# Scores by exchanged parts of q instead of k: buffers, 128-row loads, mix by quarters and an early copy of x in a hybrid attention layer

## The chip, the cores and the metric

The kernel runs on one core of a Trainium2 chip. The metric is the device time of one execution in microseconds. TensorE is called PE (its weight loads PEld), VectorE DVE, ScalarE ACT, GpSimd POOL; SP (SyncE) issues most of the transfers, POOL some of them.

## The reference

One layer: a norm, one wide projection, eight heads of differential attention and four heads of gated linear attention side by side, a gate and a norm on each, the output projection, a norm, and the residual. All arrays are float32, 1024 positions of 1024 columns.

```python
h = rms_norm(x, pre_g)
z = jnp.einsum('bsd,de->bse', h, w_in)
qa, ka, va, ga, qb, kb, vb, gb, gk_low = split_columns(z)
...
# diff_attention: q, k hold two maps of 64 columns per head
s = jnp.einsum('bqhmd,bkhmd->bhmqk', qb, k).astype(jnp.float32)   # q scaled by 64 ** -0.5
p = jax.nn.softmax(jnp.where(mask, s, -jnp.inf), axis=-1)         # causal
w = p[:, :, 0] - lam * p[:, :, 1]
out = jnp.einsum('bhqk,bkhv->bqhv', w.astype(v.dtype), v)
...
oa = rms_norm(oa, subln_g) * (1.0 - lam_init)
oa = oa.reshape(B, S, DA_WIDTH) * jax.nn.silu(ga)
ob = gla_chunked(qb, kb, vb, log_a)        # gated linear attention
ob = rms_norm(ob, gla_g) * jax.nn.silu(gb)
y = jnp.einsum('bse,ed->bsd', jnp.concatenate([oa, ob], axis=-1), w_out)
return x + rms_norm(y, post_g)
```

## The kernel before

**Two parts of every number.** A float32 value enters PE as two parts, `hi` (rounded) and `lo` (the rest); a product takes hi*hi + lo*hi + hi*lo. For the scores the two parts lie beside each other along the contracted side: a q or k of 64 columns becomes 128 rows, its hi in rows 0 to 63 and its lo in rows 64 to 127. `k` has the order hi, lo; `ks` is the same k with the order lo, hi. A score tile is `q` times `k` (hi*hi + lo*lo) plus `q` times `ks` (hi*lo + lo*hi); `q` is the stationary operand in both (`scores`, L1128).

**Stages.** First x is loaded, normed and transposed, and projected by a scheme of seven products on 2x2 blocks (`order`, `go`, `step`): the values of the linear attention (VB), those of the attention (VA), and then q, k and gates in pairs of heads. `take` (L366) splits finished q and k into parts and stores them in DRAM, in `qk_d`, laid out [part, map, 64, position]: one store for each part, 128 rows (both maps) of 512 positions, or one store for both parts in the last steps. The linear attention (`gla`) is mingled with the last projections. From about 617 us on come the heads of the attention: three streams are merged in a written order (`merge`): the scores (`all_scores`), the values (`all_values`), and the output projection of what is finished (`out_early`), which keeps PE busy between them. At the end, the partial results are summed, normed and added to x.

**Loads of a head.** `load_qk` (L979) loads one half (512 positions) of `q`, `k` or `ks` into a tile of 128 rows: two transfers of 64 rows each, one for each part, of 256 KB. A head works down from its last block of 128 queries (`qb` 7) to its first; half 1 of q serves blocks 7 to 4, half 0 blocks 3 to 0, and every block needs k from position 0 on. Even heads use the tags of the pool `kp`; odd heads have their own tiles (`smps`) for k0, k1, ks0 and q1. The tags ks1 and q0 have one buffer for all heads: ks1 is loaded once the head before has done block 4, q0 once it has done block 0.

**Output projection.** `load_mix` (L1335) loads finished attention outputs from `mixd`, four rows of tiles by 512 positions, into `m_raw`, one buffer; `mix_part` splits them. The order of output blocks is `ENDS` = 4, 5, 6, 7, 0, 1, 2, 3. `weights` (L1008) loads the output weights (`wo_hi`, `wo_lo`). The residual gets to the output by a copy of x to `out` from DRAM to DRAM, for six blocks; at the end their results are added to it by accumulating transfers. The copies are written in `out_early`, on SP (L1393).

**Order.** All matmuls, and what goes through `keep_in_program_order`, keep the order of the code; among these on SP are the last stores of q and k, the first two loads of `mix`, the last `wo` loads, and v of head 0. All else is ordered by the framework's scheduler, which follows its own model of time. Each queue then works in its fixed order.

Of the kernel before, what the change touches and what calls it, by code (L numbers as in the profile page):

```python
# [14 lines left out]
P = 128  # L15
# [16 lines left out]
def hymba_kernel(  # L32
# [181 lines left out]
    def load_early(p):  # L214

        c0 = pairs[p][2]
        r = kp.tile([P, 2, HB, P], F32, tag=f"ks{p % 2}", name="w_early")
        early[p] = [r[:, 0], r[:, 1]]
        for kh in range(2):
            rows = slice(kh * 512, kh * 512 + 512)  # L220
            sp.dma_start(r[:, kh], w_in[0, rows, c0 : c0 + P].rearrange("(k p) c -> p k c", p=P))
# [44 lines left out]
    def block_weights(i):  # L266

        kind, n, kk = order[i]
        b11, b12, b21, b22, t = (
            blocks_w.get((kind, name, kk)) for name in ("11", "12", "21", "22", "t")  # L270
        )
        w = [ap.tile([P, 2, 512], F32R, tag="ring", name="w", bufs=NRING) for _ in range(2)]
        with in_turn():
            if n == 6:
                t = kp.tile([P, 2, 512], F32, tag=f"ks{kk}", name="w_t")
# [9 lines left out]
            act.copy(w[0], src)  # L285
            split_last[:] = [dve.tensor_tensor(w[1], src, fp(w[0]), ALU.subtract)]
        ws[i] = w
        if (kind, n, kk) == ("VB", 7, 1):
            make_blocks("VA", "11", ("k0", "k1"))
            load_blocks("VA", "11")  # L290
        elif (kind, n, kk) == ("VB", 4, 1):
            make_blocks("VA", "12", None)
            make_blocks("VA", "21", None)
            make_blocks("VA", "22", ("q0", "q1"))
            load_blocks("VA", "21", "12", "22")
        elif (kind, n, kk) == ("VA", 7, 1):
            load_raw(0)
        elif (kind, n, kk) == ("VA", 4, 1):
            load_raw(1)
# [66 lines left out]
    def take(kind, n, half, unit, c):  # L366

        cs = cols(half)
        if kind in ("QA", "KA"):
            h = n + unit  # L370

            ending = made[0] > len(order) - LEAD
            both = None
            if ending and order[made[0] - 1][1] == 7:
                both = ap.tile([P, 2, 512], F32R, tag="raw", name="qk_st", bufs=4)
                hi, lo = both[:, 0], both[:, 1]
            else:
                hi, lo = t_st("qk_st", F32R), t_st("qk_st", F32R)
            scale = -0.125 if kind == "QA" else 1.0
            act.activation(hi, c, AF.Copy, scale=scale)  # L380
            dve.scalar_tensor_tensor(lo, c, scale, fp(hi), ALU.mult, ALU.subtract)
            d = qk_d["q" if kind == "QA" else "k"][h]
            if both is not None:
                tc.keep_in_program_order(
                    sp.dma_start(d[:, :, :, cs].rearrange("t m p s -> (m p) t s"), fp(both))
                )
            else:
                for t, src in enumerate((hi, lo)):
                    ins = sp.dma_start(d[t, :, :, cs].rearrange("m p s -> (m p) s"), fp(src))
                    if ending:  # L390
                        tc.keep_in_program_order(ins)
        elif kind in ("GA", "GB"):
            g = t_st("g_st")
            act.activation(g, c, AF.Exp, scale=-1.0)
            act.activation(g, g, AF.Ln, bias=1.0)
            act.activation(g, g, AF.Exp, scale=-1.0)
            dve.tensor_tensor(g, c, g, ALU.mult)
            d = g_d[n + unit] if kind == "GA" else gg_d[n][unit]
            sp.dma_start(d[:, cs], g)
        elif kind == "QB":  # L400
            g = n + unit
            e_q, _ = decs[g]
            q, qd = t_st("gq_st"), t_st("gq_st")
            dve.scalar_tensor_tensor(q, c, QSCALE, e_q[:, cs], ALU.mult, ALU.mult)
            dve.tensor_tensor(
                qd.rearrange("p (n i) -> p n i", i=P),
                q.rearrange("p (n i) -> p n i", i=P),
                dsteps[g][:, half * 4 : half * 4 + 4].unsqueeze(2).to_broadcast([P, 4, P]),
                ALU.mult,
            )  # L410
            for t, src in enumerate((q, qd)):
                sp.dma_start(gq_d[g][t, :, cs], src)
        else:
# [324 lines left out]
    gkl = kp.tile([P, S], F32R, tag="ks0", name="gkl")  # L738
    ku = kp.tile([P, 2, 512], F32R, tag="ks1", name="ku")
    up, keep = ku[:, 0], fp(ku)[:, 1]  # L740

    def low_rank():
# [94 lines left out]
    def gla_keys(n):  # L837

        g, half = n // 2, n % 2
        if g < GLA_HEADS and n not in keys:  # L840
            kq = keys[n] = kp.tile([P, 2, 512], F32, tag="ks0", name="kq")
            for i, t in enumerate((2, 0)):
                sp.dma_start(kq[:, i], gq_d[g][t, :, cols(half)])

# [36 lines left out]
    def gla():  # L881
# [6 lines left out]
        for g, half in [(g, half) for g in range(GLA_HEADS) for half in range(2)]:  # L888
# [46 lines left out]
                free.append(ib)  # L935
                yield
            yield
            gates = kp.tile([P, 2, 512], F32, tag="ks1", name="gg")
# [39 lines left out]

    def load_qk(h, n, half):  # L979

        if h % 2 and (n == "k" or (n, half) in (("ks", 0), ("q", 1))):
            t = smps[0].tile([P, 2, 512], F32R, tag=f"{n}{half}", name=f"{n}{half}")
        else:
            t = kp.tile([P, 2, 512], F32R, tag=f"{n}{half}", name=f"{n}{half}")
        for i in range(2):
            d = qk_d["q" if n == "q" else "k"][h][1 - i if n == "ks" else i, :, :, cols(half)]
            sp.dma_start(fp(t[64 * i : 64 * i + 64]), d.rearrange("m p s -> p m s"))
        qk[h, n, half] = t

    qk, smps = {}, []  # L990
# [5 lines left out]
    for _ in fill[0] if fill else ():  # L996
        pass
    fill.clear()
    for n in ("q", "k", "ks"):
        load_qk(0, n, 1)  # L1000
        if n != "q":
            load_qk(0, n, 0)
    load_qk(0, "q", 0)

    E, wo = D // P, {}
    md = mixd.rearrange("(e p) s -> p e s", p=P)
# [121 lines left out]
    def scores(h, qb):  # L1128
# [4 lines left out]
        p0 = pp.tile([P, n], F32, tag=f"p0_{qb}", name="p0", bufs=1)  # L1133
        p1 = smp.tile([P, S], F32, tag="p1", name="p1", bufs=2)
        for m, p in enumerate((p0, p1)):
            q = qk[h, "q", qb // 4][:, m, qc]
            parts = parts_of(n)
            if h == DA_HEADS - 1 and (qb, m) in ((1, 1), (0, 0), (0, 1)):

                parts = [(0, 512)]  # L1140
            for i, (a, b) in enumerate(parts):
                sc = sc_bank("sc", [P, 512])
                for j, name in enumerate(("k", "ks")):
                    for half in range(2):
                        lo, hi = max(a, half * 512), min(b, half * 512 + 512)
                        if lo < hi:
                            mm(
                                sc[:, lo - a : hi - a], q,
                                qk[h, name, half][:, m, lo - half * 512 : hi - half * 512],
                                start=(j == 0), stop=(j == 1),  # L1150
                            )
                e = min(b, n)
# [49 lines left out]
    def all_scores():  # L1202
        for h in range(DA_HEADS):
            for qb in range(NT - 1, -1, -1):
# [1 line left out]
                    yield lambda h=h, qb=qb: (h - 1, qb // 2) in used  # L1206
                yield from scores(h, qb)
                if qb == NT - 1 and h + 1 < DA_HEADS:
                    for n, half in (("q", 1), ("k", 0), ("k", 1), ("ks", 0)):
                        load_qk(h + 1, n, half)  # L1210
                if qb == 4 and h + 1 < DA_HEADS:
                    load_qk(h + 1, "ks", 1)
            if h + 1 < DA_HEADS:
                load_qk(h + 1, "q", 0)
        for _ in range(3):
            scale_scores(None)
        scored.append(True)
# [112 lines left out]

    wop = ctx.enter_context(tc.tile_pool(name="wop", bufs=1, side="right", reuse_waits="tile"))

    halves = {}

    def load_mix(st, e, n):  # L1335
        half = st // 4
        if (half, e) not in halves:
            raw = halves[half, e] = wop.tile([P, 4, 512], F32, tag="m_raw", name="m_raw", bufs=1)
            sp.dma_start(raw[:, :n, :], md[:, e : e + n, cols(half)])
        return halves[half, e][:, :, st % 4 * P : st % 4 * P + P]  # L1340

    def mix_part(st, e, n, raw=None, pool_d=None):

# [34 lines left out]
    def out_early():  # L1378
# [10 lines left out]
            pool.dma_start(yd[0][dh], y_tile(ps[dh]))  # L1389
        for st in range(1, NT - 1):  # L1390
            part, nxt = nxt, mix(st + 1)
            rows = slice(ENDS[st - 1] * P, ENDS[st - 1] * P + P)
            sp.dma_start(out[0, rows, :], x[0, rows, :])  # L1393
            for dh in range(2):
                ps = y_bank(st, dh, "ypart")
                for e in range(E, E + 8):
# [5 lines left out]
        part = nxt  # L1402
        ps = [y_bank(NT - 1, dh, "ypart") for dh in range(2)]
        load_mix(ENDS[0], 0, 4)
        for e in range(E, E + 8):
            for dh in range(2):
                times(ps[dh], part, E, dh, e, E + 7)
# [7 lines left out]
        for n, st in enumerate(ENDS):  # L1415
# [5 lines left out]
                weights(3 + n, kept)  # L1421
            if n + 1 < NT:
                nxt = mix_part(ENDS[n + 1], 0, 4)
            if n == 2:
                load_mix(ENDS[4], 0, 4)
            for dh in range(2):
                ps = y_bank(st, dh, "ypart")
                for e in range(4):
# [209 lines left out]
```

## Time and profile before

| | |
|---|---|
| Time, median of 3 runs | 1001.48 us (999.04 to 1001.82) |
| Profiled execution | 1000.23 us, span 998.5 us |
| PE busy | 963.4 us, 96% of the span |
| DVE, ACT, POOL busy | 739.4, 590.2, 207.2 us |
| Granted PE clock, mean | 0.988 |
| DMA traffic over the span | 220.37 MB, mean 221 GB/s |

The profile is of one execution. "Waited for" tells what released an engine after an idle time. In the tables by stretch, each engine has its busy time in that stretch and, in brackets, how many instructions; PEclk is the granted share of PE's full clock; the DMA share is the mean busy share of the sixteen DMA engines (a little over 1.00 is full), and GB/s what they moved. A timeline row is: start, length, engine, line, operation, tile written<-tiles read, how many. A row of the chain is: start, length, what.

### The profile page before, as it was taken

The page shows a single profiled execution, that of the slowest core. Times are in us where ns is not written, and L with a number is a line of the kernel's source. Part 1 is how long each engine was busy: PE and PEld are TensorE (multiplying, and loading weights), DVE is VectorE, ACT ScalarE, POOL GpSimd, SP SyncE. Part 2 cuts the span into 40 slices and gives each one's busy share as a digit, 9 for nine tenths or more (in the row PEclk, how much of TensorE's full clock was granted, in tenths as well). Part 3 has the DMA queues.
Part 4 walks back from the last instruction along what each step waited for, and adds up shares of the span by engine and source line. Part 5 has one row for each costly group of instructions (what it writes and reads, how often), then busy time and mean ns, then how long its engine had stood idle before and what let it go on. Part 6 is the DMA issues. An engine that isn't in the chain of part 4 may idle for free.

```text
span 998.5 us, 14800 instructions
## 1 busy us (share of the span) xinstructions
PE 963.4 (96%) x4866; PEld 812.0 (81%) x4866; DVE 739.4 (74%) x1450; ACT 590.2 (59%) x1152; POOL 207.2 (21%) x277
## 2 busy tenths in 40 slices
PE   6999999999999999999999999969999999899997
PEld 4888888778888888888888888758888888788775
DVE  5996476889899767877777784637777777677655
ACT  8641232456476467766677662537667668577664
POOL 5320000012112221211200000213322324343232
PEclk9999999999999999999999999979999999999999
DMA  8644333757857766889975679985596699984657
GB/s 299 228 146 148 127 106 94 229 190 255 299 179 244 270 206 233 273 304 307 299 242 174 189 257 357 316 232 173 161 269 177 166 285 284 296 241 89 178 149 157
DMA packets 142508, 220.37 MB, mean 221 GB/s; under 512 B 14448, under 2 KB 74864, under 8 KB 142336
## 3 DMA queue, kind: packets, MB, share of 16 engines
q1 hardware_dynamic: 128288, 178.53, 57.3%
q0 software_dynamic: 14144, 40.90, 13.8%
q8 instruction: 38, 0.62, 0.3%
q14 instruction: 38, 0.31, 0.1%
HBM read 133.93 MB, written 88.60 MB: 223 GB/s over the span
## 4 chain that ended last, share of the span: by engine, by line
PE 84%; DMA 11%; DVE 3%; ACT 2%; issue 1%; SPq 0%; DVEq 0%; POOL 0%; ACTq 0%
PE x L111 16%; PE v L111 15%; PE y L111 10%; PE z L111 10%; PE ypart L111 9%; PE sc L111 5%; PE po L111 4%; PE yps L111 4%; DMA m_raw<-mixd 3%; PE gpo L111 3%; PE wtr L114 2%; PE kv L111 1%; DMA ks<-k_d 1%; DMA q<-q_d 1%; DMA v<-v_d 1%; DMA k_d<-qk_st 1%
## 5 line engine op out<-in xcount | busy, mean ns | idle before, releaser
L1167 ACT ACTIVATE p<-p,stt 128x896 f32<-128x896 f32 (+7 forms) x128 | 99.2, 776 | 57.2 <-DVE stt L1157 44.2
L330 DVE TENSOR_TENSOR w<-w_raw,w 128x512 fp32r<-128x512 f32 x134 | 92.0, 689 | 36.2 <-ACT w L328 36.0
L328 ACT CAST w<-w_raw 128x512 fp32r<-128x512 f32 x134 | 82.7, 620 | 46.7 <-PE y L111 22.7
L1157 DVE CUSTOM_DVE_ANT_0 p<-sc,maskt 128x512 f32<-128x512 f32 (+3 forms) x128 | 74.5, 586 | 40.0 <-PE sc L111 39.2
L1193 POOL TENSOR_SCALAR p<-p,stt,lam 128x1024 f32<-128x1024 f32 (+3 forms) x64 | 56.0, 876 | 226.9 <-DVE stt L1192 222.0
L111 PE MATMUL ypart<-wo_hi,m_hi 128*128 128x512 f32 x192 | 80.4, 419 | 2.1 <-DMA wo_hi<-wo_d 1.5
L111 PE MATMUL y<-h_hi,w 128*128 128x512 f32 x320 | 80.6, 394 | 0.0
L111 PE MATMUL x<-s_hi,w 128*128 128x512 f32 x320 | 80.5, 394 | 0.0
L111 PE MATMUL z<-s_hi,w 128*128 128x512 f32 x320 | 80.4, 393 | 0.0
L111 PE MATMUL v<-w,s_hi 128*128 128x512 f32 x256 | 79.0, 389 | 0.1
L111 PE MATMUL sc<-k,q 128*128 128x512 f32 (+1 forms) x192 | 72.5, 380 | 6.1 <-DVE stt L1157 6.1
L111 PE MATMUL sc<-ks,q 128*128 128x512 f32 (+1 forms) x192 | 68.0, 356 | 9.4 <-DMA ks<-k_d 9.4
L111 PE MATMUL ypart<-wo_lo,m_hi 128*128 128x512 f32 x192 | 76.6, 399 | 0.5 <-DMA wo_lo<-wo_d 0.5
L111 PE MATMUL ypart<-wo_hi,m_lo 128*128 128x512 f32 x192 | 76.3, 398 | 0.0
L479 ACT COPY s<-x 128x512 f32<-128x512 f32 x60 | 35.1, 584 | 65.3 <-PE x L111 65.1
L111 PEld LDWEIGHTS z<-s_hi,w 128*128 128x128 f32 x320 | 59.1, 188 | 11.7
L111 PEld LDWEIGHTS x<-s_hi,w 128*128 128x128 f32 x320 | 59.1, 188 | 11.7
L111 PEld LDWEIGHTS y<-h_hi,w 128*128 128x128 f32 x320 | 59.0, 188 | 11.7
L285 ACT CAST w<-w_block 128x1024 fp32r<-128x1024 f32 x24 | 25.0, 1051 | 66.3 <-PE v L111 43.2
L257 DVE TENSOR_TENSOR w_raw<-w_raw 128x512 f32<-128x512 f32 x80 | 55.2, 690 | 9.8 <-DMA w_raw<-in_w_in_dram 8.8
L111 PE MATMUL v<-w,h_hi 128*128 128x512 f32 x192 | 60.3, 401 | 0.4 <-ACT h_hi L573 0.4
L1235 ACT CAST wt_hi<-wtr 128x512 fp32r<-128x512 f32 (+1 forms) x80 | 43.1, 538 | 25.6 <-PE wtr L114 24.6
(231 smaller groups left out, 2392.3 us busy)
## 6 DMA issues: line engine op xcount, KB each, us to landing
w_raw<-in_w_in_dram SPq DMA_DIRECT2D x40, 512.0 KB, 5.0
w_block<-in_w_in_dram SPq DMA_DIRECT2D x16, 512.0 KB, 4.2
wo_raw<-in_w_out_dram POOLq DMA_DIRECT2D x32, 256.0 KB, 4.2
wo_d<-wo_hi POOLq DMA_DIRECT2D x32, 256.0 KB, 4.3
wo_d<-wo_raw POOLq DMA_DIRECT2D x32, 256.0 KB, 5.1
ks<-k_d SPq DMA_DIRECT2D x32, 256.0 KB, 8.0
k<-k_d SPq DMA_DIRECT2D x32, 256.0 KB, 8.7
q<-q_d SPq DMA_DIRECT2D x32, 256.0 KB, 8.6
```

The source lines that it names most:

```text
L111: tc.keep_in_program_order(pe.matmul(*a, **k))
L114: tc.keep_in_program_order(pe.transpose(dst, src, ident))
L257: dve.tensor_tensor(dst, a, b, ALU.subtract)
L285: act.copy(w[0], src)
L328: act.copy(w[0], src)
L330: split_last[:] = [dve.tensor_tensor(w[1], src, fp(w[0]), ALU.subtract)]
L479: act.copy(b[k], ps)
L1157: ins = dve.tensor_tensor_reduce(p[:, a:e], sc[:, : e - a], maskt[:, NZ + P - (e - a) :] if last else maskt[:, : e - a], 1.0, 3e38 if i == ...
L1167: act.activation(p[:, :n], p[:, :n], AF.Exp, bias=st[:, m : m + 1], scale=-1.0, accum_out=st[:, 2 + m : 3 + m],)
L1193: pool.tensor_scalar(p1[:, :n], p1[:, :n], st[:, 5:6], lam, ALU.mult, ALU.mult)
L1235: act.copy(hi[:, :n], pt[:, :n])
```

## The change

- Scores: the exchanged operand is now q. `qs` is q with the parts in the order lo, hi; a score tile is `q` times `k` plus `qs` times `k`, with q and qs as stationary operands.
- Buffers: odd heads have their own tiles for k0, k1, q1 and qs1, so that all that a head's blocks 7 to 4 need has two buffers; q0 and qs0 have one, and are loaded once the head before has done block 0. The tags ks0 and ks1, which earlier stages use too, are now called qs0 and qs1.
- Layout: `qk_d` is [map, part, 64, position]. `q` and `k` are loaded by one transfer of 128 rows, `qs` by two of 64. Every store of q or k is split in two, one for each map, of 64 rows.
- `load_mix` loads quarters (256 positions) into two buffers, and asks for some of them earlier.
- The six copies of x to `out` are issued by POOL, and written among the steps of the VA stage.

```diff
@@ load_early (and the same tag in block_weights, gkl, ku, gla_keys, gates)
-        r = kp.tile([P, 2, HB, P], F32, tag=f"ks{p % 2}", name="w_early")
+        r = kp.tile([P, 2, HB, P], F32, tag=f"qs{p % 2}", name="w_early")
@@ block_weights
             load_blocks("VA", "21", "12", "22")
+        elif (kind, n) in (("VA", 1), ("VA", 2), ("VA", 6)):
+            st = {1: 4, 2: 6, 6: 0}[n] + kk
+            pool.dma_start(out[0, st * P : st * P + P, :], x[0, st * P : st * P + P, :])
@@ take
             if both is not None:
-                tc.keep_in_program_order(
-                    sp.dma_start(d[:, :, :, cs].rearrange("t m p s -> (m p) t s"), fp(both))
-                )
+                for m in range(2):
+                    tc.keep_in_program_order(
+                        sp.dma_start(
+                            d[m, :, :, cs].rearrange("t p s -> p t s"), fp(both)[64 * m : 64 * m + 64]
+                        )
+                    )
             else:
                 for t, src in enumerate((hi, lo)):
-                    ins = sp.dma_start(d[t, :, :, cs].rearrange("m p s -> (m p) s"), fp(src))
-                    if ending:
-                        tc.keep_in_program_order(ins)
+                    for m in range(2):
+                        ins = sp.dma_start(d[m, t, :, cs], fp(src)[64 * m : 64 * m + 64])
+                        if ending:
+                            tc.keep_in_program_order(ins)
@@ load_qk
-        if h % 2 and (n == "k" or (n, half) in (("ks", 0), ("q", 1))):
+        if h % 2 and (n == "k" or half):
...
-        for i in range(2):
-            d = qk_d["q" if n == "q" else "k"][h][1 - i if n == "ks" else i, :, :, cols(half)]
-            sp.dma_start(fp(t[64 * i : 64 * i + 64]), d.rearrange("m p s -> p m s"))
+        d = qk_d["k" if n == "k" else "q"][h][:, :, :, cols(half)]
+        if n != "qs":
+            sp.dma_start(fp(t), d.rearrange("m t p s -> (t p) m s"))
+        else:
+            for i in range(2):
+                sp.dma_start(fp(t[64 * i : 64 * i + 64]), d[:, 1 - i].rearrange("m p s -> p m s"))
@@ loads of head 0
-    for n in ("q", "k", "ks"):
-        load_qk(0, n, 1)
-        if n != "q":
-            load_qk(0, n, 0)
-    load_qk(0, "q", 0)
+    for n, half in (("q", 1), ("k", 1), ("k", 0), ("qs", 1), ("q", 0), ("qs", 0)):
+        load_qk(0, n, half)
@@ scores
-                for j, name in enumerate(("k", "ks")):
+                for j, name in enumerate(("q", "qs")):
...
-                                sc[:, lo - a : hi - a], q,
-                                qk[h, name, half][:, m, lo - half * 512 : hi - half * 512],
+                                sc[:, lo - a : hi - a], qk[h, name, qb // 4][:, m, qc],
+                                qk[h, "k", half][:, m, lo - half * 512 : hi - half * 512],
@@ all_scores
-                    for n, half in (("q", 1), ("k", 0), ("k", 1), ("ks", 0)):
+                    for n, half in (("q", 1), ("k", 0), ("k", 1), ("qs", 1)):
                         load_qk(h + 1, n, half)
-                if qb == 4 and h + 1 < DA_HEADS:
-                    load_qk(h + 1, "ks", 1)
             if h + 1 < DA_HEADS:
-                load_qk(h + 1, "q", 0)
+                for n in ("q", "qs"):
+                    load_qk(h + 1, n, 0)
@@ load_mix
-        half = st // 4
-        if (half, e) not in halves:
-            raw = halves[half, e] = wop.tile([P, 4, 512], F32, tag="m_raw", name="m_raw", bufs=1)
-            sp.dma_start(raw[:, :n, :], md[:, e : e + n, cols(half)])
-        return halves[half, e][:, :, st % 4 * P : st % 4 * P + P]
+        part = st // 2
+        if (part, e) not in parts_m:
+            raw = parts_m[part, e] = wop.tile([P, 4, 256], F32, tag="m_raw", name="m_raw", bufs=2)
+            sp.dma_start(raw[:, :n, :], md[:, e : e + n, part * 256 : part * 256 + 256])
+        return parts_m[part, e][:, :, st % 2 * P : st % 2 * P + P]
@@ out_early
-            rows = slice(ENDS[st - 1] * P, ENDS[st - 1] * P + P)
-            sp.dma_start(out[0, rows, :], x[0, rows, :])
...
         load_mix(ENDS[0], 0, 4)
+        load_mix(ENDS[2], 0, 4)
...
-            if n == 2:
-                load_mix(ENDS[4], 0, 4)
+            if n % 2 == 0 and n + 4 < NT:
+                load_mix(ENDS[n + 4], 0, 4)
...
         mix_pair(0)
+        load_mix(ENDS[2], 4, 3)
```

More of the change, by code (lines that the diff above doesn't have):

```diff
@@ L274, in block_weights @@
             if n == 6:
-                t = kp.tile([P, 2, 512], F32, tag=f"ks{kk}", name="w_t")
+                t = kp.tile([P, 2, 512], F32, tag=f"qs{kk}", name="w_t")
                 blocks_w[kind, "t", kk] = t
@@ L737, in hymba_kernel @@
     go(2)
-    gkl = kp.tile([P, S], F32R, tag="ks0", name="gkl")
-    ku = kp.tile([P, 2, 512], F32R, tag="ks1", name="ku")
+    gkl = kp.tile([P, S], F32R, tag="qs0", name="gkl")
+    ku = kp.tile([P, 2, 512], F32R, tag="qs1", name="ku")
     up, keep = ku[:, 0], fp(ku)[:, 1]
@@ L840, in gla_keys @@
         if g < GLA_HEADS and n not in keys:
-            kq = keys[n] = kp.tile([P, 2, 512], F32, tag="ks0", name="kq")
+            kq = keys[n] = kp.tile([P, 2, 512], F32, tag="qs0", name="kq")
             for i, t in enumerate((2, 0)):
@@ L937, in gla @@
             yield
-            gates = kp.tile([P, 2, 512], F32, tag="ks1", name="gg")
+            gates = kp.tile([P, 2, 512], F32, tag="qs1", name="gg")
             for t in range(2):
@@ L1135, in scores @@
         for m, p in enumerate((p0, p1)):
-            q = qk[h, "q", qb // 4][:, m, qc]
             parts = parts_of(n)
@@ L1331, in hymba_kernel @@
     wop = ctx.enter_context(tc.tile_pool(name="wop", bufs=1, side="right", reuse_waits="tile"))
-    halves = {}
+    parts_m = {}
     def load_mix(st, e, n):
-        half = st // 4
-        if (half, e) not in halves:
-            raw = halves[half, e] = wop.tile([P, 4, 512], F32, tag="m_raw", name="m_raw", bufs=1)
-            sp.dma_start(raw[:, :n, :], md[:, e : e + n, cols(half)])
-        return halves[half, e][:, :, st % 4 * P : st % 4 * P + P]
+        part = st // 2
[3 more added lines that the diff above has]
+        return parts_m[part, e][:, :, st % 2 * P : st % 2 * P + P]
     def mix_part(st, e, n, raw=None, pool_d=None):
```

## Prediction

> **What bounds the kernel now.** I read the page's head first, then the waits of PE, then the stretches around each wait, and last the queues.
>
> ```profile
> span 998.5 us, 14800 instructions
> PE 963.4 (96%) x4866; PEld 812.0 (81%) x4866; DVE 739.4 (74%) x1450; ACT 590.2 (59%) x1152; POOL 207.2 (21%) x277
> ...
> PEclk9999999999999999999999999979999999999999
> DMA  8644333757857766889975679985596699984657
> ```
>
> PE is busy 96% of the span, so about 35 us of idle are all that a reordering can win, apart from slices at a lower clock. The waits of PE say where:
>
> ```profile
> PE sc L111 <- DMA ks<-k_d: 9.4, 1, 9.4
> PE xT L114 <- DVE x L532: 8.9, 4, 7.4
> PE sc L111 <- DVE stt L1157: 6.1, 4, 3.5
> PE ypart L111 <- DMA wo_hi<-wo_d: 1.5, 1, 1.5
> ...
> PE ypart L111 <- DMA wo_lo<-wo_d: 0.5, 1, 0.5
> ```
>
> One wait of 9.4 us is for a `ks` tile, the thing that the change double-buffers; one of 3.5 us stands behind DVE's score statistics; two, 2.0 us together, are for `wo` weights; 8.9 us lie at the start. The stretches show what moved meanwhile:
>
> ```profile
> core 0: us, PE busy (x) PEld busy (x) DVE busy (x) ACT busy (x) POOL busy (x), PEclk, DMA share, GB/s
> 7.00:14.00 7.00, 4.75 (x17) 3.18 (x18) 5.43 (x15) 6.81 (x16) 3.67 (x4) 1.00 1.04 370
> 612.00:620.00 8.00, 7.90 (x35) 6.19 (x35) 5.35 (x8) 2.91 (x5) 0.00 (x0) 1.00 1.05 292
> 620.00:628.00 8.00, 8.00 (x37) 6.66 (x36) 4.35 (x14) 2.63 (x5) 0.02 (x1) 1.00 1.07 335
> 628.00:633.00 5.00, 2.98 (x12) 1.91 (x12) 2.20 (x5) 2.02 (x4) 1.18 (x1) 0.99 1.01 411
> 656.60:666.00 9.40, 0.03 (x2) 0.04 (x1) 0.12 (x2) 0.46 (x1) 0.00 (x0) 0.69 1.03 207
> 666.00:668.00 2.00, 2.00 (x5) 1.61 (x6) 1.21 (x4) 0.36 (x1) 0.28 (x1) 0.50 1.00 226
> 668.00:671.00 3.00, 3.00 (x13) 2.63 (x12) 0.91 (x3) 0.88 (x2) 0.18 (x1) 0.59 0.69 177
> ...
> 872.00:874.00 2.00, 2.00 (x9) 1.83 (x8) 2.00 (x6) 2.00 (x5) 0.00 (x0) 0.50 1.09 357
> 874.00:878.00 4.00, 4.00 (x22) 3.40 (x21) 0.91 (x5) 2.35 (x5) 1.98 (x2) 0.84 0.96 233
> ```
>
> Three things are to be seen. From 612 to 668 us the DMA engines are full (share 1.00 to 1.07), so there a transfer's cost is its engine time. Full engines move 411 GB/s from 628 to 633, where tiles of 128 rows land, and 207 from 656.6 to 666, where the loads are `q`, `k` and `ks` in 64 rows. And after a long wait PE runs at half its clock: 0.50 and 0.59 for the five microseconds behind the 9.4, 0.50 and 0.84 behind the 3.5.
>
> The chain of waits and SP's queue say how that stretch is paced:
>
> ```profile
> 611.09 10.06 DMA k_d<-qk_st
> 621.23 9.47 DMA wo_hi<-wo_d
> 653.55 12.30 DMA ks<-k_d
> ```
>
> ```profile
> 611.09 1.60 SPq L385 DMA_DIRECT2D k_d<-qk_st  x2
> 614.52 2.38 SPq L385 DMA_DIRECT2D q_d<-qk_st  x2
> 617.54 1.35 SPq L389 DMA_DIRECT2D k_d<-qk_st  x2
> 619.28 1.08 SPq L389 DMA_DIRECT2D q_d<-qk_st  x2
> 621.23 0.32 SPq L1021 DMA_DIRECT2D wo_hi<-wo_d  x1
> ...
> 639.63 2.98 SPq L987 DMA_DIRECT2D ks<-k_d  x2
> ...
> 652.62 1.50 SPq L987 DMA_DIRECT2D ks<-k_d  x2
> ```
>
> The `wo_hi` of 621.23 is issued when the store of 611.09 lands (611.09 + 10.06), eight issues before it: SP has eight transfers under way and waits for the oldest. The `ks` that PE waits for is issued at 652.62, four microseconds before PE needs it, and its second half takes 12.30 to land.
>
> **The change, part by part.** *Exchanged parts of q.* A score tile still takes the same matmuls of the same shapes, each with its own weight load. Stationary and moving operands change roles only in the second half of the products: 0. The first scores of head 0 now need `qs1` at once, where they needed `ks0`; that slot's load is issued where `ks1` was. A lateness there would be the same queue as in the store term below, not a second price.
>
> *Two buffers for what a head begins with.* Head 1's `qs1` has its own tile, so it is issued in one go with q1, k0 and k1, where `ks` of half 0 is issued now: in the row of 639.63, 13 us ahead of that of 652.62. The 9.4 us go, and with them the half-clock stretch: 2.0 x 0.50 + 3.0 x 0.41 = 2.2. Together -11.6. Late next are q0 and qs0, loaded only when a head has done its last block; they are needed after the four largest blocks of the next, more than half a head later. I cost them at 0; landings of 12.30 us fit in that cover.
>
> *Stores in 64 rows.* Each store of q or k becomes two (0.32 us an issue, by the row of `wo_hi`; before 612 no wait of PE is for SP's transfers). In the full stretch this lies on the path: the eight stores from 611.09 to 620.4 (four of 512 KB, four of 256 KB, 3.1 MB) become sixteen, pinned ahead of the `wo` loads for which PE already waits 2.0 us; four more of 256 KB (1.05 MB) come shortly before. No 64-row store is in the trace. From below: they keep the 335 GB/s of 620 to 628, and only q0's load, in 128 rows, gains (0.52 MB at 207 is 2.5 us, at 411 it is 1.3): -1.2. From above: 4.2 MB at 207 instead of 335 GB/s is 20.3 against 12.5: +7.8. The mixed stretch 612 to 620 (292) would give 14.4 - 12.5 - 1.2, about +0.7. The nearest row is that of the 64-row loads, alternating halves as these stores do; with q0's gain it gives +6.6. I take +5, toward it, since the loads mix in. PE waits that much longer at 629 us.
>
> [...]
>
> *q and k in 128 rows.* Half as many issues, and 411 in place of 207 GB/s, for 2 MB a head. Outside the stretches above PE waits for no q or k, so 0.
>
> *Mix by quarters, two buffers.* The 3.5 us wait behind DVE comes from here:
>
> ```profile
> ACT m_hi L1351 <- DMA m_raw<-mixd: 6.9, 2, 4.6
> ```
>
> ACT stands 4.6 us for the one `m_raw` buffer's second half, DVE and PE behind it. With two buffers of 256 columns the quarter for block 4 of the order is requested two blocks earlier. The 3.5 us go, and the half clock after it: 2.0 x 0.50 + 4.0 x 0.16 = 1.6. Together -5.1. The four extra issues cost SP under half a microsecond each, on a queue that nobody waits for there.
>
> *x to the output.* These six copies, 512 KB each, stand late in the program, and yet:
>
> ```profile
> 0.79 1.81 SPq L527 DMA_DIRECT2D x<-in_x_dram  x4
> ...
> 3.42 2.06 SPq L239 DMA_DIRECT2D w_block<-in_w_in_dram  x2
> ...
> 22.39 5.44 SPq L1393 DMA_DIRECT2D out_dram<-in_x_dram  x6
> ```
>
> The scheduler issues what depends on nothing as soon as its queue is free, here at 22.39, behind all the loads of the start. PE works without a pause from 13.68 to 617, so they cost nothing now. On POOL the queue is free much sooner:
>
> ```profile
> 1.60 0.19 POOL L155 MEMSET first_t<- 128x1 f32 x4
> 7.00 0.89 POOL L532 TENSOR_SCALAR x<-x,ssq 128x512 f32<-128x512 f32 x1 [5.21 <-DVE ssq L1602]
> ```
>
> POOL idles 5.2 us there, and the copies fit: I expect them at about 2 us, not in the stage where the code has them. POOL itself is hardly delayed (six issues took SP 5.44 us, pauses between them included); the queue that they meet is SP's, with x, `w_block` and the second half of x. Those are just in time:
>
> ```profile
> 12.01 1.04 ACT w L285
> ...
> 13.68 6.40 PE v L111 x17
> ```
>
> ```profile
> 22.40:36.60 14.20, 14.20 (x77) 12.08 (x76) 12.29 (x23) 11.51 (x23) 7.16 (x6) 1.00 0.61 227
> ```
>
> From 22.4 to 36.6 us the copies are nearly alone: 0.61 x 14.2 = 8.7 us of all sixteen engines. The engines are full from 7 to 14 (1.04), so what is served ahead of the second `w_block` delays PE's start one for one: 0 if the copies wait behind the loads or find another gap, 8.7 if all come first (a gain is excluded, since PE has no pause behind 13.68 that they could have caused). The loads have a start of one microsecond and two queues share; I take +5.5, some two thirds.
>
> [...] With all of the copies ahead of the loads the sum would be about 998.5. No run here shows copies beside those loads.
>
> **Sum**, against the profiled execution's own 1000.2 us (1.3 below the median of the three runs, 1001.5): +5.5 (start) +5.0 (stores) -11.6 (head 1) -5.1 (mix) = -6.2, so 994; carried to the median, 995.
>
> **The rivals.**
> 1. *The copies do not meet the loads* (POOL takes them later). For it: the code puts them in the v stage, slices 4 to 7, where the DMA line reads 4 and 3. Against: the row of 22.39. Then -11.7: 990, or 984 with the stores at their lower end.
> 2. *Both costs at their upper ends*: 8.7 + 7.8 - 11.6 - 5.1 = -0.2: 1001, no change. For it: 207 GB/s, and the share of 1.04 at the start. Against: 292 GB/s in the mix.
> 3. *Head 1's wait is of bytes, not of order* (slower). The engines are full until 668, so `qs1`, issued earlier, might still land no sooner. For it: share 1.03 all through the wait. Against: the eight transfers that stand ahead of the row of 652.62 would stand behind `qs1`. Then 11.6 come back: 5.5 + 5.0 - 5.1 = +5.4: 1007. It decides, against the rest of the sum, from some 9 us of wait and half clock.
>
> **How the numbers follow.** Forecast 0.48, rival 1 0.15, rival 2 0.21, rival 3 0.16. About 0.3% (3 us) is what a measurement of this kernel can tell from no change, so faster is below 998.5, slower above 1004.5. Faster: 0.15 and nine tenths of 0.48, 0.58. Same: 0.21 and 0.05, less a little of rival 2 that ends above, 0.24. Slower: 0.18. The forecast's own range is 989 to 999. The range goes from 986 (most of rival 1) to 1004 (rival 2), leaving out rival 3 and the lowest of rival 1.
>
> **What would show it.** The copies on POOL's timeline near 2 us, and PE's first `v` at about 19 instead of 13.68. PE's wait for `wo_hi` grown from 1.5 to some 6 us near 635. No wait of PE for `qs`, and PEclk without the 5 to 10 us at half near 660. No wait of ACT for `m_raw` near 870. The prediction is wrong if PE starts at 13.7 (rival 1), if `qs` shows among PE's waits with more than 5 us (rival 3), or if a wait appears on a `q` or `qs` of half 0.

## The result and the profile after

The changed kernel takes 996.87 us in the median (991.22 to 999.88), the kernel before, beside it, 1002.67 us (997.77 to 1009.9): a ratio of 0.9941, 95% interval 0.9922 to 0.996. It is faster by some 6 us, and the predicted 995 is 2 us off. The way there is another one than the prediction's, though.

The profiled execution took 998.37 us (before: 1000.23). Its page begins:

```profile
span 996.7 us, 14823 instructions
PE 960.9 (96%) x4866; PEld 809.9 (81%) x4866; DVE 738.8 (74%) x1450; ACT 591.2 (59%) x1152; POOL 210.8 (21%) x283
...
DMA  9354514568865876799986668997864858995758
```

The waits of PE (us in total, times, longest):

```profile
PE xT L114 <- DVE x L539: 17.3, 4, 7.5
PE v L111 <- ACT w L285: 2.8, 1, 2.8
PE gms L111 <- DVE gqd L974: 2.6, 1, 2.6
PE xT L114 <- POOL xt L539: 2.5, 2, 1.7
PE ypart L111 <- DMA m_hi<-mixe: 1.2, 1, 1.2
PE ypart L111 <- DMA m_lo<-mixe: 0.9, 2, 0.6
```

The 9.4 us for `ks` and the 3.5 us behind DVE's statistics are gone, and no wait for `qs` has come. In their place the wait for the first tiles of x has grown from 8.9 to 17.3 us, two more follow it (2.8 and 2.5), and there is one near 512 us that the kernel before does not have. POOL and SP at the start:

```profile
1.74 3.14 POOL L298 DMA_DIRECT2D out_dram<-in_x_dram  x6
3.46 9.93 SPq L239 DMA_DIRECT2D w_block<-in_w_in_dram  x2
13.44 4.76 SPq L534 DMA_DIRECT2D xt<-in_x_dram  x4
```

The stretches where head 1 and the last quarter begin (PE's clock third from the end):

```profile
674.00:677.00 3.00, 3.00 (x20) 2.55 (x19) 2.84 (x10) 1.50 (x5) 0.19 (x1) 1.00 1.07 385
872.00:876.00 4.00, 4.00 (x25) 3.49 (x24) 4.00 (x10) 2.88 (x6) 1.03 (x2) 1.00 1.07 289
```

PE works through both at full clock (1.00), where before it had 0.50 to 0.84. The copies are issued at 1.74 us, as forecast; SP, which needed 2.06 us for its two `w_block` issues, now stands in them for 9.93.

PE does the same 4866 instructions in the same order in both kernels, so the n-th instruction's start after, less its start before, is a running account: it says how late the changed kernel is there, and each step in it is a cost or a gain with its place. Behind the first row it is read where it is level again, after the stretch at half clock that follows a wait (in the changed kernel 0.50 from 640 to 642 us, behind the waits for `m_hi` and `m_lo` that end by 638.60).

| place (before's time) | predicted | account after the place | step |
|---|---|---|---|
| first `v`, 13.68 us | | +10.9 | +10.9 |
| second half of x, 29 to 31 us | +5.5 | +14.7 | +3.8 |
| group statistic, 495 to 498 | 0 | +19.1 | +4.4 |
| last stores and first `wo`, 612 to 638 | +5.0 | +19.0 | -0.1 |
| head 1's first `qs`/`ks`, 666 to 680 | -11.6 | +7.3 | -11.7 |
| `m_raw`, 871 to 876 | -5.1 | +1.8 | -5.5 |
| last head, 937 to 941 | 0 | -1.9 | -3.7 |
| end | -6.2 | -1.8 | +0.1 |

The two gains came as forecast. The start cost 14.7 where 5.5 was forecast and 8.7 the bound (the 5.5 stood for the start as a whole, the first two rows). The stores cost nothing in the balance where 5 was forecast: within that row the account rises by 3.5 at PE's waits for `m_hi` and `m_lo` and falls by 3.7 where only the kernel before waits for `wo`. And two places were not in the sum at all.

### The profile page after: what moved, and what is told of

Same layout as the page of the kernel before. It is cut to its first block, busy times and chain, and to the rows that moved or that the text cites. A ratio compares the mean times of both kernels' runs of the same rounds, so it can differ in the third digit from the quotient of the medians.

```text
span 996.7 us, 14823 instructions
## 1 busy us (share of the span) xinstructions
PE 960.9 (96%) x4866; PEld 809.9 (81%) x4866; DVE 738.8 (74%) x1450; ACT 591.2 (59%) x1152; POOL 210.8 (21%) x283
## 3 DMA queue, kind: packets, MB, share of 16 engines
q0 software_dynamic: 14336, 44.05, 14.7%
## 4 chain that ended last, share of the span: by engine, by line
PE 87%; DMA 6%; DVE 2%; ACT 2%; issue 2%; SPq 0%; POOL 0%; DVEq 0%; ACTq 0%; POOLq 0%
PE x L111 16%; PE v L111 15%; PE ypart L111 11%; PE y L111 11%; PE z L111 10%; PE sc L111 6%; PE po L111 5%; PE yps L111 4%; PE wtr L114 3%; PE gpo L111 2%; DMA m_lo<-mixe 2%; DMA x<-in_x_dram 2%; PE kv L111 1%; DMA mixd<-o 1%; DMA m_raw<-mixd 1%
## 5 line engine op out<-in xcount | busy, mean ns | idle before, releaser
L111 PEld LDWEIGHTS x<-s_hi,w 128*128 128x128 f32 x320 | 59.1, 188 | 11.7
L111 PEld LDWEIGHTS z<-s_hi,w 128*128 128x128 f32 x320 | 59.1, 188 | 11.6
L111 PE MATMUL sc<-k,qs 128*128 128x512 f32 (+1 forms) x192 | 66.6, 349 | 0.0
L1203 DVE SCALAR_TENSOR_TENSOR p<-p,stt,p 128x1024 f32<-128x1024 f32 (+3 forms) x64 | 52.3, 819 | 6.9 <-POOL p L1199 6.7
```

What stands on the lines that cost most here:

```text
L111: tc.keep_in_program_order(pe.matmul(*a, **k))
L1203: dve.scalar_tensor_tensor(p0[:, :n], p0[:, :n], st[:, 4:5], p1[:, :n], ALU.mult, ALU.subtract)
```

## The experiments

Ratios are to the kernel before, run beside each kernel on the same chip; it had medians of 998 to 1000 us there.

**1. Is it the copies?** Three kernels. In the first, the changed kernel's copies go back to SP:

```
-        elif (kind, n) in (("VA", 1), ("VA", 2), ("VA", 6)):
-            ...
-            pool.dma_start(out[0, st * P : st * P + P, :], x[0, st * P : st * P + P, :])
...
             part, nxt = nxt, mix(st + 1)
+            rows = slice(ENDS[st - 1] * P, ENDS[st - 1] * P + P)
+            sp.dma_start(out[0, rows, :], x[0, rows, :])
```

> The changed kernel with one part undone: the six copies of x to the output are issued by SP again, at the place in the code where the kernel before has them. Theory (the copies on POOL at 1.74 us take the DMA engines from the loads of the start): PE's first v falls back from 24.5 us to about 13.7, the half clock ends near 18.5 us, and the 14.2 us by which PE's order of work is late at 44 us of the changed kernel go: 982 to 985 us, 1.4% below the changed kernel. Rival A (the lateness at the start comes from the order in which the scheduler now puts ACT's and POOL's work there, not from the copies): PE's first v stays above 20 us and the time at 995 to 998. Rival B (the copies cost what the prediction said, 5.5 us, the rest being other edits): about 991.

Measured 980.05 us, ratio 0.9804 (0.9763 to 0.9844), two under the theory's range. The second is the kernel before with the opposite edit alone:

> The kernel before with one part of the change alone: the six copies are issued by POOL in the v stage's code, as in the changed kernel. Theory (the copies take the engines from the first loads): POOL issues them near 2 us, PE's first v comes at about 24.5 us instead of 13.68, and the time is about 14 us longer, 1015 to 1018. Rival A (order of ACT's and POOL's work): no change, 1000 to 1004, with the first v at 13.7. Rival B (5.5 us, as predicted): 1008.

Measured 1014.83 us, ratio 1.0154 (1.0107 to 1.0202). The third leaves the copies on POOL, but issues them behind its last sum of the `s4` group (`with tc.issue_after(last_sum[0].ins):` around the copy):

> The changed kernel with the copies still on POOL, but made to be issued behind POOL's last sum of the s4 group, some 55 us into the span, when the loads of the start have landed. Theory: it is when they are issued that costs, not the queue: PE's first v at about 13.7 us, 982 to 986 us, as with the copies on SP. Rival (copies on POOL's queue disturb loads or POOL's own work whenever they run): 3 to 10 us of new waits of PE for POOL or for SP's loads between 55 and 80 us, 987 to 995.

Measured 986.93 us, ratio 0.9865 (0.9822 to 0.9907). The waits of PE in the first (copies on SP):

```profile
span 977.6 us, 14816 instructions
...
PE xT L114 <- DVE x L536: 9.0, 4, 7.6
PE ypart L111 <- DMA m_lo<-mixe: 1.5, 2, 0.7
```

and in the second (only the copies moved):

```profile
PE xT L114 <- DVE x L535: 16.9, 4, 6.9
PE sc L111 <- DMA ks<-k_d: 7.1, 1, 7.1
PE sc L111 <- DVE stt L1160: 6.6, 2, 4.4
PE v L111 <- ACT w L285: 2.8, 1, 2.8
PE xT L114 <- POOL xt L535: 2.5, 2, 1.7
```

With the copies alone, all three waits of the changed kernel's start appear with nearly its numbers, and the account is level at +14.2 from 46 us on (+14.7 there). With the copies on SP they are gone: first `v` at 13.82. So the start's 14 us are the copies' and nothing else's, and both rivals of it fall. Issued late from POOL they cost little at first (first `v` at 14.37 us, 1.5 us in the account by 20): it is when they are issued, not the queue. The 7 us between 980 and 987 (8.9 between the two profiled executions) are, in the account, +3.4 by 74 us, +4.6 near 495 (on which below) and +0.8 later. The kernel with the copies on SP is the fastest of all: 1.96% under the kernel before.

**2. Bytes, or a queue that is full?** Three copies on POOL and three on SP:

```
-        elif (kind, n) in (("VA", 1), ("VA", 2), ("VA", 6)):
+        elif (kind, n, kk) in (("VA", 1, 0), ("VA", 1, 1), ("VA", 2, 0)):
```

> The changed kernel with only three of the six copies on POOL at the start (rows 4 to 6 of eight); the other three are issued by SP as in the kernel before. Theory (the copies are served ahead of the loads, and their bytes push PE's start back one for one): PE's first v about half as late, at 18.5 to 20 us instead of 13.8 (none) or 24.5 (six), and 986 to 990 us. Rival (what costs is that SP stands 9.14 us in one issue once more than a certain number of transfers are under way, whoever owns them): with three copies SP's issue of the first w_block takes under 2 us, the first v comes near 14 to 16 us, and the time is 980 to 984.

Measured 988.06 us, ratio 0.9875 (0.9836 to 0.9914); first `v` at 19.91 us, 6.1 late; the account to the kernel with the copies on SP is +7.3 at 78 us, where six copies have +15.0. Half the copies, half the cost, 7.3 us for 1.57 MB and 15.0 for 3.15: here it went with their bytes. SP stood 5.83 us in its first `w_block` issue here too, so that is a sign, not a threshold.

**3. Who goes first on a shared engine?** In the changed kernel the copies go in 16 pieces of 32 KB, the x tiles in 128 rows of 4 KB. What the two queues had of the sixteen engines from 6 to 17.7 us (POOL's is q0, SP's q1; share of the engines last):

```profile
q0 software_dynamic: 190, 3.08, 70.9%
q1 hardware_dynamic: 1260, 0.82, 25.1%
```

The third tile of x, issued at 1.71 us, lands at 11.54, and the fourth, issued at 2.18, at 17.86, behind the last copy (17.66). The same copies in rows of 2 KB:

```
+            o_st, x_st = (
+                d[0, st * P : st * P + P, :].rearrange("p (c k) -> c p k", k=512) for d in (out, x)
+            )
-            pool.dma_start(out[0, st * P : st * P + P, :], x[0, st * P : st * P + P, :])
+            pool.dma_start(o_st, x_st)
```

> The changed kernel with the six copies on POOL at the same place, each cut by columns so that it goes in rows of 2 KB instead of 16 pieces of 32 KB (512 KB either way). Theory P (the engines take turns between queues piece by piece, so the large pieces of POOL's queue are what shuts out SP's rows of 4 and 2 KB): the third and fourth tile of x, which land at 11.5 and 17.9 us in the changed kernel, land by 8.5 and 11, PE's first v by 20 us at the latest, and the time is 987 to 993. Theory Q (POOL's queue or the earlier request goes first whatever the size of its pieces): first v at 24 to 25 us, 995 to 998. Theory R (small pieces make the copies dearer): later than 25 us and over 1000.

Measured 1002.91 us, ratio 1.0025 (1.0 to 1.0049); the profiled execution took 998.54. Its trace has the copies in pieces of 4 KB, 768 in all, with short ones of 8 bytes between them. x landed at 7.26 and 9.12 us, as theory P has it, but the first `v` came at 22.07 and the time is theory R's. The queues' shares from 9.2 to 19 us, and the waits of PE:

```profile
q1 hardware_dynamic: 841, 1.82, 57.5%
q0 software_dynamic: 2624, 1.40, 50.5%
```

```profile
PE xT L114 <- DVE x L542: 8.9, 4, 7.8
PE v L111 <- ACT h_hi L583: 8.7, 1, 8.7
PE xT L114 <- POOL xt L542: 8.2, 2, 7.6
```

Now the two queues have the engines in about equal parts, POOL's 50.5% and SP's 57.5% with the copies in pieces of 4 KB, where it was 70.9% and 25.1% with pieces of 32 KB: the share went with the size of the pieces. Turns of one piece each, as in theory P, the counts do not show: in the first window SP's queue had 229 pieces of 4 and 2 KB beside POOL's 94 of 32 KB. The delay had only moved. On ACT the cast of the first `w_block` stands ahead of the `h_hi` that PE waits for, and it is late:

```profile
20.39 1.04 ACT L285 CAST w<-w_block 128x1024 fp32r<-128x1024 f32 x1 [9.17 <-DMA w_block<-in_w_in_dram]
```

That `w_block` lands at 20.36, right behind the gain `pre_g`, 4 KB in elements of 4 bytes, which SP issues just ahead of it and which lands at 19.08 (8.81 in the kernel before). Loading the gain first:

```
+    sp.dma_start(pre_g, pre_norm_g[0].rearrange("(k p) -> p k", p=P))
     for st in range(4):
         load_x(st)
-    sp.dma_start(pre_g, pre_norm_g[0].rearrange("(k p) -> p k", p=P))
```

> The kernel with the copies on POOL in rows of 2 KB, with one more edit: the load of the gain pre_g, 1024 elements of 4 bytes each, is issued ahead of the four tiles of x instead of behind them. In the run with small pieces, x landed at 7.3 and 9.1 us but pre_g only at 19.1, ten microseconds after the tile in front of it (0.45 us without copies). Theory (an engine serves the queues in turn, one piece each, whatever the sizes: 1024 / 16 = 64 pieces of 4 bytes wait 64 times for a piece of 2 KB, some 10 us): pre_g, now ahead of the copies, lands before 6 us; x at 8 to 10 us; the first w_block near 12 to 13 and the second near 15, as SP's rows of 2 KB and POOL's take turns; PE's first v at 15 to 18 us instead of 22; the copies take until 30 us or more. Rival (small loads are late beside the copies for another reason, a late issue or a late completion): pre_g or w_block again lands near 19 us, first v at 20 us or later.

Measured 998.36 us, ratio 0.9973 (0.995 to 0.9996). `pre_g` landed at 3.04, x at 8.22 and 10.55, the first `v` came at 16.19: the theory's numbers, with the `w_block` later than it said (14.48 and 18.41). (Neither one piece for each queue in turn nor its count of 64 turns is shown: in the kernel without this edit SP's queue moved 1.82 MB from 9.2 to 19 us, while `pre_g` was under way, so later loads went past it.) Yet by 48 us the account against the changed kernel is +0.8. PE's waits and POOL's timeline say where the gain of 8.4 us at the first `v` went:

```profile
PE xT L114 <- POOL xt L542: 10.5, 2, 9.9
PE xT L114 <- DVE x L542: 9.8, 3, 8.8
```

```profile
26.18 2.23 POOL L542 TENSOR_SCALAR xt<-xt,ssq 128x1024 f32<-128x1024 f32 x2 [2.60 <-ACT ssq L1601]
39.81 2.21 POOL L542 TENSOR_SCALAR xt<-xt,ssq 128x1024 f32<-128x1024 f32 x2 [11.39 <-ACT lams L830]
```

The second half of x is scaled at 39.81, in the changed kernel at 40.03 (POOL stands 7.29 us there for ACT's `f1lo`, an instruction ahead of the norm on ACT). What the copies delay is a whole train of loads; PE can be served earlier at its head and then stands further back. That the order of ACT's instructions in front of that norm holds the last 3.8 us of the 14.7 is read from these rows; it was not tried by itself.

**4. The layout of q and k.** The changed kernel with the copies on SP, stores in 128 rows and loads in 64 again:

```
-                for m in range(2):
-                    ... sp.dma_start(d[m, :, :, cs].rearrange("t p s -> p t s"), fp(both)[64 * m : 64 * m + 64])
+                ... sp.dma_start(d[:, :, :, cs].rearrange("t m p s -> (m p) t s"), fp(both))
...
-        if n != "qs":
-            sp.dma_start(fp(t), d.rearrange("m t p s -> (t p) m s"))
-        else:
-            ...
+        for i in range(2):
+            part = 1 - i if n == "qs" else i
+            sp.dma_start(fp(t[64 * i : 64 * i + 64]), d[part].rearrange("m p s -> p m s"))
```

> The copies on SP, and the stores of q and k in 128 rows and the loads of q and k in 64 rows again, as in the kernel before (two loads for each tile); the exchange of q, the second buffers and the mix by quarters stay. Against the kernel with only the copies moved back to SP this isolates the layout. Theory from the changed kernel's trace (3.1 MB of 64-row stores land in 7.7 us at the end of projection, so they run at no lower rate): within 2 us of it, 981 to 987 us, PE's wait at the first wo tile within 1.5 us. Rival (the prediction's term, 64-row stores cost 5 us): about 5 us faster than it, 977 to 980. Rival (64-row loads of head 1 land too late for PE): a wait for qs or k of 3 to 9 us near 660 and 986 to 993 us.

Measured 981.37 us, ratio 0.9816 (0.9772 to 0.986), against 0.9804 with the new layout on the same chip: no difference beyond the noise, and not the 5 us less that the prediction's term asks for. The term is refuted. In the changed kernel's stretch of stores (us, then busy time by engine, PE's clock, DMA share, GB/s):

```profile
636.00:640.00 4.00, 2.18 (x8) 1.31 (x7) 1.38 (x2) 0.63 (x1) 0.00 (x0) 0.90 1.04 404
640.00:642.00 2.00, 2.00 (x6) 1.60 (x5) 0.00 (x0) 0.00 (x0) 0.00 (x0) 0.50 1.06 400
```

Eight stores of 256 KB in 64 rows, on alternating halves, land from 640.47 to 644.93, behind a load that lands at 639.80: 2.1 MB in 5.13 us, 409 GB/s. That is twice the 207 GB/s that the prediction carried over from the 64-row loads. The kernel before's own stores, all of 128 rows, already show a high and a low rate with full engines:

```profile
622.50:624.00 1.50, 1.50 (x8) 1.25 (x7) 0.91 (x3) 0.00 (x0) 0.00 (x0) 1.00 1.05 404
624.50:626.00 1.50, 1.50 (x8) 1.26 (x7) 1.27 (x4) 1.44 (x3) 0.00 (x0) 1.00 1.07 228
```

In that kernel the last 3.1 MB of stores land within 9.5 us of the load ahead of them (619.98 to 629.47); in 64 rows, in the changed kernel, within 7.75 (639.80 to 647.55). So the low rate, 207 and 228 GB/s, is no matter of 64 rows alone; what makes it, no run shows. Whether 64-row loads are slower than 128-row ones stays open too: no transfer of either kind was timed by itself.

**5. The buffers, alone and taken away.** The kernel before with only the exchange and the second buffers:

> The kernel before with only the exchanged parts of q and the second buffers for what a head begins with: stores in 128 rows, loads in 64 rows, mix in halves, copies on SP, all as before. Theory (prediction's 11.6 us, 9.4 of wait and 2.2 of half clock, and no other part needed for it): 1.2% under the kernel before, 984 to 989 us, no wait for qs or ks. Rival (the loads in 128 rows are needed too, since 64-row loads at 207 GB/s land too late): a wait of 3 to 6 us for k or qs near 660, 990 to 995.

Measured 988.75 us, ratio 0.9879 (0.9844 to 0.9914): no wait for `ks` or `qs`, an account of -11.2 behind head 1's start. And the fast kernel (copies on SP) with one buffer for `qs1`:

```
-        if h % 2 and (n == "k" or half):
+        if h % 2 and (n == "k" or (n, half) == ("q", 1)):
...
-                    for n, half in (("q", 1), ("k", 0), ("k", 1), ("qs", 1)):
+                    for n, half in (("q", 1), ("k", 0), ("k", 1)):
                         load_qk(h + 1, n, half)
+                if qb == 4 and h + 1 < DA_HEADS:
+                    load_qk(h + 1, "qs", 1)
```

> The copies on SP, and one buffer for qs1, which head 1's is then loaded into behind head 0's block 4, as the ks of half 1 was in the kernel before; the exchange of q and all else stay. Against the kernel with only the copies moved back (980) this measures the second buffer. Theory (order, not bytes): PE waits 8 to 10 us for qs near 655, with 2 us of half clock behind it: 989 to 993. Rival (bytes: what came before in 64 rows and now comes in 128 rows has made room, so the late load still lands in time, and the second buffer is worth nothing): no wait over 2 us for qs, 979 to 982.

Measured 989.91 us, ratio 0.9895 (0.9852 to 0.9938), 10 us more than 980.05. Its largest wait of PE that the fast kernel lacks:

```profile
PE sc L111 <- DMA qs<-q_d: 7.4, 2, 4.1
```

The wait is back, in two places (660 and 816 us; +6 and +5 in the account, with the lower clock behind it, 0.57 from 660 to 664 us) instead of one: a miss in form, not in sum. The wait is of order. Rival 3 of the prediction falls with these two runs.

**6. The mix.** The fast kernel with the mix in halves and one buffer again:

```
-            raw = parts_m[part, e] = wop.tile([P, 4, 256], F32, tag="m_raw", name="m_raw", bufs=2)
-            sp.dma_start(raw[:, :n, :], md[:, e : e + n, part * 256 : part * 256 + 256])
+            raw = halves[half, e] = wop.tile([P, 4, 512], F32, tag="m_raw", name="m_raw", bufs=1)
+            sp.dma_start(raw[:, :n, :], md[:, e : e + n, cols(half)])
```

> The copies on SP, and the mix loaded in two halves of 512 columns into one buffer again, as in the kernel before; the exchange of q, the second buffers and the layout stay. Against the kernel with only the copies moved back (980) this measures the mix edit. Theory (the prediction's 5.1 us: 3.5 of wait and 1.6 of half clock, in the last head): ACT waits over 4 us for m_raw, PE waits 3 to 4 us for DVE's statistics near 860, 984 to 987 us. If the wait of 2.1 us near 937 of the kernel before came from the same buffer, it is back too: 987 to 989. Rival (the wait hung on the order that the one buffer for ks left, not on m_raw): no wait over 2 us for the statistics, 979 to 982.

Measured 984.5 us, ratio 0.9854 (0.981 to 0.9897): the edit is worth some 4.4 us (single times of 982.82 to 990.41 against 977.67 to 982.78), and the account puts it at two places, +2.4 near 856 and +1.0 near 919. ACT waits only 2.7 us for `m_raw`, not over 4, and PE 1.6 us near 856, not 3 to 4. With the old layout as well (the kernel of 5 with only the buffers) the same two places cost +6.8 and +2.4, half clock included; against the old layout with quarters (981.37) the mix is then worth 7.4. By these numbers the layout, worth nothing by itself, makes the wait smaller that the quarters remove; the intervals of 4.4 and 7.4 overlap, so this is not shown.

The place near 937 us of the kernel before is another thing. DVE's and POOL's timelines there:

```profile
933.67 3.02 DVE L1461 TENSOR_TENSOR m_lo<-m_raw,m_hi 128x384 fp32r<-128x384 f32 x1
...
936.96 0.55 DVE L1461 TENSOR_TENSOR m_lo<-m_raw,m_hi 128x384 fp32r<-128x384 f32 x1
```

```profile
933.94 1.60 POOL L1290 TENSOR_TENSOR o<-r,gate 128x512 f32<-128x512 f32 x1
935.22 1.06 POOL L1193 TENSOR_SCALAR p<-p,stt,lam 128x512 f32<-128x512 f32 x1
```

The same subtraction takes 3.02 us while POOL's two run, and 0.55 after them; in all four kernels with the mix in halves one of that line takes 3.02 to 3.03, in the nine with quarters none takes over 0.72. PE's 2.1 us and its half clock (0.50 from 937.1 to 940 us) hang on that one. What makes it long the rows do not show: in the changed kernel a subtraction of that line takes 0.55 us at 935.38 beside a row of POOL's (`p`, 935.34, 1.15 us). By quarters the casts come at other times, and none comes out long; the author's reading is a gain by chance of order.

**7. Whose is the wait near 512 us?** The changed kernel, copies on POOL, with the old layout of q and k:

> The changed kernel, copies on POOL at the start as in it, with the stores of q and k in 128 rows and their loads in 64 rows as in the kernel before. What it tells: whose is the wait of PE for the group statistic gqd near 512 us (2.6 us and 2.2 of half clock), which the changed kernel has and the one with the copies on SP has not. There ACT stands 2.87 us for a store of q, which then landed about 3 us later. Theory (the doubled stores of q on SP's queue, together with the later start's other phase): the wait is gone, 990 to 993 us. Rival (the scheduler's order with the copies on POOL alone): the wait stays, 995 to 998, equal to the changed kernel.

Measured 996.07 us, ratio 0.9951 (0.9929 to 0.9974). The wait for `gqd` is gone (4.4 us less in the account, with the lower clock behind it, 0.66 and 0.77 from 512 to 518 us of the changed kernel), yet the time is the changed kernel's. Against it the start is 1.2 us later; two waits for `wo` weights near 647 us take back the 3.5 us gained ahead of them, where PE does not wait for `m_hi` and `m_lo`; a third near 836 costs 1.6; and the account ends at -1.9. The time is missed. The mechanism agrees with this one trace, but is not shown by it: the kernel with small pieces has the doubled stores and the late start, and no such wait. ACT's waits around it in the changed kernel, then in the fast one:

```profile
ACT g_st L401 <- DMA q_d<-qk_st: 2.9, 1, 2.9
```

```profile
ACT g_st L398 <- DMA q_d<-qk_st: 0.2, 1, 0.2
```

ACT stands for a store of q that is still under way (2.9 and 0.2 us), and the statistic is queued behind. Which of the stores ahead makes that landing late in some kernels (the held copies, three copies, the small pieces with the gain first) and not in others (small pieces alone) stays open.

## Why the prediction was right, and where it was not

- **Start, +5.5 (0 to 8.7): right in mechanism, size missed by far.** The copies were at 1.74 us and did meet the loads. The step that failed is the bound: it took the copies' engine time, 0.61 x 14.2 = 8.7 us, as the most that PE could lose. PE's first `v` lost 10.9, and the second half of x, late behind the same train, let PE stand twice more, +3.8. "Two queues share" was read as a discount; with pieces of 32 KB against 4 KB the copies had 71% of the engines and came first in all but name. Its sign for this, the first `v` at about 19, came at 24.54.
- **Stores, +5 (-1.2 to +7.8): wrong, measured -0.1.** It is inside the bounds, near the value by the mixed stretch (+0.7) that was passed over for the 64-row loads. The step that failed is to read 207 GB/s as a property of 64 rows: 64-row stores landed at 409, stores in 128 rows went at 228 in one stretch of the kernel before, and in the stretch of 207 itself three transfers of 128 rows land too (a `gate`, `m_lo` and `m_hi`, at 658.03, 660.07 and 662.41). The sign, a wait for `wo_hi` of 6 us near 635, did not come; two of `m_hi` and `m_lo`, 2.1 us together, stand there instead.
- **Head 1, -11.6: right**, -11.7 in the account, -11.2 alone, +10 when undone.
- **Mix, -5.1: right in size at its place** (-5.3 from 871 to 876 us; the other 0.2 of its row came before), and worth 4.4 to 7.4 by what stands beside it.
- **Not in the sum:** +4.4 near 495 and -3.7 near 937.

Rows of the account add up to -1.8, the medians differ by 5.8; the profiled execution of before was 2.4 us under its median, the one of after 1.5 over. So the sum of the steps, -6.2, met the median since an excess of 9.2 at the start stood against 5.1 at the stores, the two unforeseen places nearly against each other (+0.7), and the rest against the scatter of single executions. That the total came out is luck: of its four terms only the two gains came as reckoned. Rival 1, copies that do not meet the loads, is what the fast kernel is: 980, under both values given (990 and 984), because the stores are free and the last head gains 3.7.

## What to carry to other kernels

A transfer that depends on nothing was issued here where its queue first fell idle, whatever the place in the code (at 22.39 us on SP, at 1.74 on POOL): put it behind something, or on a queue whose earlier work holds it back, as SP's loads did. Between the two queues the share went with the size of the pieces (70.9% to 25.1% with copies in pieces of 32 KB, 50.5% to 57.5% with 4 KB); a bulk copy in 32 KB pieces beside a start of small rows cost 10.9 us at PE's first `v`, where its engine time was an estimated 8.7 (0.61 x 14.2), and 3.8 by what the late train set off behind it. And a rate read from one stretch belongs to that stretch's mix (207 GB/s beside 64-row loads, 409 for 64-row stores, 404 and 228 for stores in 128 rows): before it becomes the price of a new form of transfer, look for the same form elsewhere, and for the same rate with other forms.

## What the runs showed of the hardware that was not expected

- Large pieces of one queue against rows of another: 70.9% to 25.1% of the engines; with the copies in pieces of 4 KB, 50.5% to 57.5%. A load of 4 KB in elements of 4 bytes landed 16.4 us after its issue beside them, and 2.2 us when it was issued ahead of them.
- 64-row stores on alternating halves: 409 GB/s. Stores in 128 rows, in the kernel before: 404 GB/s, and 228 a microsecond later.
- One DVE subtraction of 128x384 beside two POOL instructions: 3.02 us, and 0.55 once they had ended; what made it long was not shown.
